# Newton steps and scaled x of a norm in PSUM, norms interleaved with the products that remain, and copies moved between engines, in a two-layer hybrid diffusion backbone

## Chip, cores and metric

One NeuronCore of one Trainium2 chip. The metric is the device time of one execution in microseconds, the median of several runs. Most executions of one kernel agree within 0.3%.

## What is computed

Two layers run over 512 latent tokens and 256 context tokens of width 1024, in fp32:

```python
for l in range(2):
    sh1, sc1, g1, sh2, sc2, g2 = modulation(c, ada_w[l], ada_b[l], 6)   # silu(c) @ ada_w + ada_b
    # the context has its own six from c_ctx; in the last layer only the first two
    hx = modulate(x, norm1_g[l], sh1, sc1)        # rms_norm(x, g) * (1 + scale) + shift
    hc = modulate(xc, norm1_g[l], csh1, csc1)
    ux, uc = hx @ w_in[l], hc @ w_in[l]           # keys, values, queries, pool input, gates
    # mixers: multi-scale pooling, 2-D neighbourhood attention, windowed attention with sinks,
    # latent attention; latent queries read latent and context keys, context reads context only
    mixed = sum(sigmoid(gate_i) * (y_i @ w_branch[i])) @ w_out
    x = x + g1 * mixed
    x = x + g2 * ((silu(h @ w1) * (h @ w3)) @ w2)    # h = modulate(x, norm2_g, sh2, sc2)
    # the context stream gets the same two updates, except in the last layer
return rms_norm(x, final_norm_g)
```

## The kernel before

Activations lie transposed: eight tiles of 128 channels by 768 tokens, 512 latent ones (piece `PL`) and 256 context ones (piece `PC`). Each fp32 operand is split in a high part and the rest, and a product is three matmuls (`mm3`, L149 to L151): high x high, rest x high, high x rest. A weight slab is loaded by SyncE's queue into `wraw` (three buffers), converted by ScalarE to the high part (L143) and subtracted by GpSimd to the rest (L157; the tiles `gatelo`, `wolo`, `w1lo` and so on; four buffers each).

The order of TensorE's work is made by a `Stream` of jobs. A job is a generator that emits some matmuls and then yields the microseconds that they should take; when a job starts, the weights of the next one are loaded. `st.defer(us, fn, key)` has `fn` emitted once the jobs have passed that much product time, `st.need(key)` emits it at once. Attention is emitted between pieces of jobs (`st.drive`). The framework then lays out each engine's queue ahead of the run: earlier emitted instructions come first when their inputs should be ready. SyncE's queue keeps the emitted order.

The parts that the change touches:

- **adaLN work.** `ada_run(n)` takes n steps of the generator that computes the modulation vectors. After the first four groups, a group is eight loads of a 128x512 weight block (`adaraw`) with one or two VectorE products each into PSUM (`adaacc`, tag `sc`; L397, L399), and a transpose and a reduction for each accumulator (L406, L407). Nine `adaraw` blocks have room, and up to eight are loaded ahead. `cur["side"]` is the number of steps for each four k tiles of a product, from the second job of the fourth gate on 1.2, in the FFN 0.75. Layer 0's second norm needs groups up to the sixth.
- **Norm.** `Norm.squares` adds up squares as x is updated (L468, L469). `stats` sums over channels on TensorE (`ps_ssq`, L476), computes the reciprocal root by three Newton rounds on columns (`newton`, L442 to L448, VectorE) and writes a diagonal `dg` (L480). `apply` spreads it by a matmul (`ps_rstd`, L487), then per k scales x on VectorE (`nh`, L514), adds the shift on ScalarE (L517, L521) and writes the two halves `hh` and `hl` (L519 by GpSimd or VectorE, L522 by VectorE).
- **PSUM.** Eight banks: tag `mm` three, `sc` two, `tr` two, `pv` one. `ps_ssq` and `ps_rstd` take `tr`; so do output products of the second piece.
- **Projections.** `project_jobs` has eight output tiles m. For the output projection (b = 16) and the last part of w2 (b = 40), tiles 4 to 7 do the first piece only, and four `tail` jobs then do the rest. `stats(first)` follows the first tail, `apply(first)` the second. The pieces are `PL`, `PC` in layer 0 and two halves of 256 tokens in layer 1.
- **First FFN job.** `first_ffn_job` does hidden tile 0 for the first piece, then the other piece's norm, then that piece.
- **Entry of layer 1.** `mix` emits the pool products, and after them the context norm's `apply` and the token-major products (`tm`).
- **Mixers.** `split_k` puts each key half into both partition halves (L956, L957); the pool branch sums windows (L741, L743); `na_bias` adds a mask to a bias block in three instructions per head (L1010).

## Time and profile before

| | us |
|---|---|
| Median of 3 runs | 2248.66 (2248.55 to 2250.43) |
| The profiled execution, among them | 2250.43 |
| Its span | 2248.6 |

| Engine | busy us | share of the span |
|---|---|---|
| TensorE, matmuls | 2153.3 | 96% |
| VectorE | 1298.7 | 58% |
| ScalarE | 878.3 | 39% |
| GpSimd | 723.7 | 32% |

The granted TensorE clock was 0.985 of full speed over the span. In the rows, PE is TensorE, PEld its weight loads, DVE VectorE, ACT ScalarE, POOL GpSimd, SPq the load queue of SyncE. Times in a row of instructions are from the span's start; L is a line of the kernel.

### The profile page before, as it was taken

To read this page: it belongs to the slowest core of one execution; us is meant where nothing else is said; L and a number is where in the kernel's file an instruction comes from. 1 tells how busy PE (TensorE), PEld (TensorE's weight loads), DVE (VectorE), ACT (ScalarE), POOL (GpSimd) and SP (SyncE) were. 2 spreads that over 40 slices of the span, in tenths; PEclk is the share of its full clock that TensorE was granted. 3 is DMA by queue.
4 is the path that set the end of the run, shared out by engine and by line. 5 is a ranking of instruction groups with operands and counts; after the bars stand their busy time and mean duration, and the time that the engine had idled before them with its cause. 6 is when DMAs were issued, how large, how long until landed. Compare 5 with 4: busy or idle time off the path is not lost.

```text
span 2248.6 us, 32590 instructions
## 1 busy us (share of the span) xinstructions
PE 2153.3 (96%) x11792; PEld 1840.8 (82%) x11792; DVE 1298.7 (58%) x2935; ACT 878.3 (39%) x1973; POOL 723.7 (32%) x591
## 2 busy tenths in 40 slices
PE   6999999999999899999999998998999988999998
PEld 2878888888888788888888877877887787888886
DVE  6774667767789877644412266667777444212225
ACT  4354555544432422122122334555655334323233
POOL 1322222222222323333333323323233353444443
PEclk9999999999999899999999999999999999999999
DMA  7422111112454334445422223322222232333332
GB/s 240 111 60 57 43 50 43 45 45 64 125 166 147 109 124 140 141 133 154 126 69 60 89 83 103 87 57 59 59 66 69 82 115 64 98 95 96 99 100 89
DMA packets 317333, 211.59 MB, mean 94 GB/s; under 512 B 17370, under 2 KB 284916, under 8 KB 317172
## 3 DMA queue, kind: packets, MB, share of 16 engines
q1 hardware_dynamic: 308756, 201.65, 31.1%
q10 hardware_dynamic: 8416, 7.87, 1.0%
q8 instruction: 93, 1.52, 0.3%
q14 instruction: 68, 0.56, 0.1%
HBM read 202.90 MB, written 6.55 MB: 93 GB/s over the span
## 4 chain that ended last, share of the span: by engine, by line
PE 77%; DVE 12%; DMA 3%; ACT 2%; issue 2%; POOL 1%; SPq 0%; ACTq 0%; POOLq 0%; DVEq 0%
PE ps_w L150 13%; PE ps_w L149 13%; PE ps_w L151 13%; PE ps_gate L149 5%; PE ps_gate L151 5%; PE ps_gate L150 5%; PE pv L869 3%; PE tr L855 2%; DMA gater<-in_w_in_dram 1%; DVE adaacc L399 1%; PE ps_y L149 1%; PE ps_y L150 1%; PE ps_y L151 1%; PE ps_wo L151 1%; PE ps_wo L150 1%
## 5 line engine op out<-in xcount | busy, mean ns | idle before, releaser
L157 POOL TENSOR_TENSOR gatelo<-gater,gatehi 128x512 fp32r<-128x512 f32 x128 | 172.5, 1351 | 461.0 <-ACT gatehi L143 439.4
L149 PE MATMUL ps_gate<-hh,gatehi 128*128 128x512 f32 (+1 forms) x768 | 278.9, 363 | 1.4 <-ACT gt L808 1.4
L151 PE MATMUL ps_gate<-hh,gatelo 128*128 128x512 f32 (+1 forms) x768 | 274.3, 357 | 0.8 <-POOL gatelo L157 0.6
L150 PE MATMUL ps_gate<-hl,gatehi 128*128 128x512 f32 (+1 forms) x768 | 274.0, 357 | 0.0
L399 DVE SCALAR_TENSOR_TENSOR adaacc<-adaraw,cs,adaacc 128x512 f32<-128x512 f32 x224 | 160.5, 749 | 77.3 <-DMA adaraw<-in_ada_w_dram 76.2
L149 PE MATMUL ps_w<-hh,w1hi 128*128 128x512 f32 (+1 forms) x504 | 179.4, 356 | 0.0
L149 PE MATMUL ps_w<-hh,w3hi 128*128 128x512 f32 (+1 forms) x504 | 178.7, 355 | 0.0
L150 PE MATMUL ps_w<-hl,w1hi 128*128 128x512 f32 (+1 forms) x504 | 178.5, 354 | 0.0
L150 PE MATMUL ps_w<-hl,w3hi 128*128 128x512 f32 (+1 forms) x504 | 178.5, 354 | 0.0
L151 PE MATMUL ps_w<-hh,w1lo 128*128 128x512 f32 (+1 forms) x504 | 178.3, 354 | 0.0
L151 PE MATMUL ps_w<-hh,w3lo 128*128 128x512 f32 (+1 forms) x504 | 178.3, 354 | 0.0
L157 POOL TENSOR_TENSOR w3lo<-w3r,w3hi 128x512 fp32r<-128x512 f32 x84 | 110.6, 1322 | 191.1 <-ACT w3hi L143 189.3
L157 POOL TENSOR_TENSOR w1lo<-w1r,w1hi 128x512 fp32r<-128x512 f32 x84 | 108.6, 1294 | 190.2 <-ACT w1hi L143 187.6
L149 PE MATMUL ps_w<-gh,w2hi 128*128 128x512 f32 (+1 forms) x472 | 165.6, 351 | 0.0
L151 PE MATMUL ps_w<-gh,w2lo 128*128 128x512 f32 (+1 forms) x472 | 165.3, 350 | 0.0
L150 PE MATMUL ps_w<-gl,w2hi 128*128 128x512 f32 (+1 forms) x472 | 165.2, 350 | 0.0
L151 PEld LDWEIGHTS ps_gate<-hh,gatelo 128*128 128x128 f32 x768 | 145.5, 189 | 21.6 <-POOL gatelo L157 1.6
L149 PEld LDWEIGHTS ps_gate<-hh,gatehi 128*128 128x128 f32 x768 | 145.7, 190 | 19.7 <-ACT gt L808 2.3
L150 PEld LDWEIGHTS ps_gate<-hl,gatehi 128*128 128x128 f32 x768 | 146.0, 190 | 16.9
L157 POOL TENSOR_TENSOR w2lo<-w2r,w2hi 128x512 fp32r<-128x512 f32 (+1 forms) x80 | 97.5, 1224 | 157.1 <-ACT w2hi L143 155.7
L1497 DVE SCALAR_TENSOR_TENSOR ft<-ft,ps_w 128x512 f32<-128x512 f32 (+1 forms) x67 | 39.4, 589 | 145.5 <-ACT ft L1496 145.4
L143 ACT ACTIVATE gatehi<-gater 128x512 fp32r<-128x512 f32 x128 | 80.4, 630 | 96.9 <-DMA gater<-in_w_in_dram 33.6
(420 smaller groups left out, 5615.3 us busy)
## 6 DMA issues: line engine op xcount, KB each, us to landing
adaraw<-in_ada_w_dram SPq DMA_DIRECT2D x160, 256.0 KB
gater<-in_w_in_dram SPq DMA_DIRECT2D x128, 256.0 KB
w1r<-in_ffn_w_dram SPq DMA_DIRECT2D x84, 256.0 KB
w3r<-in_ffn_w_dram SPq DMA_DIRECT2D x84, 256.0 KB
w2r<-in_ffn_w_dram SPq DMA_DIRECT2D x56, 256.0 KB
ada<-in_ada_w_dram SPq DMA_DIRECT2D x32, 256.0 KB
wbr<-in_w_branch_dram SPq DMA_DIRECT2D x64, 128.0 KB
wor<-in_w_out_dram SPq DMA_DIRECT2D x32, 256.0 KB
```

What stands on the lines that cost most here:

```text
L143: nc.scalar.activation(out=o, in_=i, func=AF.Copy, scale=scale)
L149: nc.tensor.matmul(ps, ah, bh, start=start, stop=False)
L150: nc.tensor.matmul(ps, ah, bl, start=False, stop=False)
L151: return nc.tensor.matmul(ps, al, bh, start=False, stop=stop).ins
L157: cur["lo"].tensor_tensor(out=lo, in0=raw, in1=hi.bitcast(F32), op=ALU.subtract)
L399: nc.vector.scalar_tensor_tensor(out=acc[j], in0=raw, scalar=c, in1=acc[j], op0=ALU.mult, op1=ALU.add)
L855: nc.tensor.transpose(tr[:, 128 * j:128 * j + 128], ps[qi][0][:, c0:c0 + 128], ident)
L869: nc.tensor.matmul(acc[:, 128 * q0:128 * (q0 + nq)], v[rows], t[rows, c:c + 128 * nq], start=(i == 0), stop=(i == nmm - 1))
L1497: nc.vector.scalar_tensor_tensor(out=t, in0=t, scalar=1.0, in1=p1, op0=ALU.add, op1=ALU.mult)
```

## The change

The Newton steps keep `y` and the shifted integer in the columns behind the sums, in the same PSUM bank. The scaled x of `apply` goes to PSUM (tag `sc`, two banks) and every k takes the two-instruction form. `stats` and `apply` of the first piece are deferred by 2.0 and 5.5 us from the end of the last tile's first piece. The first FFN job becomes six: hidden tile 0 and hidden tile 1 for the first piece, tile 1 and then tile 0 for the second. The context norm at the entry to layer 1 is deferred by 2.0 us into the pool products. adaLN steps run at 1.4 in place of 1.2 and stop at six groups until hidden tile 1 is done for the first piece. Squares are deferred by 1.5 us. One key copy and the pool branch's copy go from VectorE to ScalarE, the bias additions from VectorE to GpSimd, and two of four heads' bias blocks are loaded and added 24 us later.

```diff
@@ -179,7 +179,7 @@
     st = Stream()
-    cur = {"ada": None, "side": 0.0, "credit": 0.0, "groups": 0, "after": None, "lo": nc.gpsimd, "wants": (1.3, 2.0, 1.3, 1.4)}
+    cur = {"ada": None, "cap": 6, "side": 0.0, "credit": 0.0, "groups": 0, "after": None, "lo": nc.gpsimd, "wants": (1.3, 2.0, 1.3, 1.4)}
@@ -194,7 +194,8 @@
                     cur["credit"] -= 1
-                    ada_run(1)
+                    if cur["groups"] + (cur["ada"] is not None) < cur["cap"]:
+                        ada_run(1)
                 yield min(n, step) * 3 * (s1 - s0) / 2400
@@ -435,13 +436,16 @@
-    def newton(src, n, mean):
+    def newton(src, n, mean, room=None):
         v, y, t = (cp.tile([128, 8], F32, tag=f"nw{c}", name=f"nw{c}", bufs=2)[:, :n] for c in "vyt")
+        g = t
+        if room is not None:
+            y, g = room[:, 0:n], room[:, n:2 * n]
         V = nc.vector
         V.tensor_scalar(out=v, in0=src, scalar1=mean, scalar2=EPS, op0=ALU.mult, op1=ALU.add)
-        V.tensor_scalar(out=t.bitcast(I32), in0=v.bitcast(I32), scalar1=1, scalar2=None, op0=ALU.logical_shift_right)
-        V.tensor_scalar(out=y.bitcast(I32), in0=t.bitcast(I32), scalar1=-1, scalar2=0x5F3759DF, op0=ALU.mult, op1=ALU.add)
+        V.tensor_scalar(out=g.bitcast(I32), in0=v.bitcast(I32), scalar1=1, scalar2=None, op0=ALU.logical_shift_right)
+        V.tensor_scalar(out=y.bitcast(I32), in0=g.bitcast(I32), scalar1=-1, scalar2=0x5F3759DF, op0=ALU.mult, op1=ALU.add)
         for _ in range(3):
@@ -471,10 +475,10 @@
         nt = n // 128
-        ps = psum("tr", "ps_ssq", 2 * nt)
+        ps = psum("tr", "ps_ssq", 6 * nt)
         for t in range(nt):
             nc.tensor.matmul(ps[:, 2 * t:2 * t + 2], acc[:, 128 * t:128 * t + 128], ones[:, 0:2], start=True, stop=True)
-        r = newton(ps, 2 * nt, mean)
+        r = newton(ps[:, 0:2 * nt], 2 * nt, mean, ps[:, 2 * nt:6 * nt])
         dg = tmp([128, n], F32, "dg")
@@ -510,16 +514,11 @@
                 sh, sc = (mods[self.l][:, b + k, cond:cond + 1] for b in self.b)
-                t = tmp([128, n], F32, "nh")
+                t = psum("sc", "nh", n)
                 nc.vector.scalar_tensor_tensor(out=t, in0=cur["x"][k][:, s0:s1], scalar=sc, in1=rstd, op0=ALU.mult, op1=ALU.mult)
                 hh, hl = (t_[:, s0:s1] for t_ in cur["h"][k])
-                if k % 2:
-                    nc.scalar.activation(out=t, in_=t, func=AF.Identity, bias=sh)
-                    act_copy(hh, t)
-                    (nc.gpsimd if k == 1 else nc.vector).tensor_tensor(out=hl, in0=t, in1=hh.bitcast(F32), op=ALU.subtract)
-                else:
-                    nc.scalar.activation(out=hh, in_=t, func=AF.Identity, bias=sh)
-                    nc.vector.scalar_tensor_tensor(out=hl, in0=t, scalar=sh, in1=hh.bitcast(F32), op0=ALU.add, op1=ALU.subtract)
+                nc.scalar.activation(out=hh, in_=t, func=AF.Identity, bias=sh)
+                nc.vector.scalar_tensor_tensor(out=hl, in0=t, scalar=sh, in1=hh.bitcast(F32), op0=ALU.add, op1=ALU.subtract)
@@ -740,7 +739,7 @@
                     if j >= both:
-                        nc.vector.tensor_copy(dst[0:64, 8:n + 8], prev[0:64, 8:n + 8])
+                        act_copy(dst[0:64, 8:n + 8], prev[0:64, 8:n + 8])
                     prev = dst
@@ -953,7 +952,7 @@
                 sub_hi(dst[1], src, dst[0])
-                nc.vector.tensor_copy(kd[e][o, s0:s1], kd[e][r, s0:s1].bitcast(F32))
+                act_copy(kd[e][o, s0:s1], kd[e][r, s0:s1].bitcast(F32))
                 nc.vector.tensor_copy(kl[e][o, s0:s1], kl[e][r, s0:s1].bitcast(F32))
@@ -1007,7 +1006,7 @@
                 for v, (j0, nj) in enumerate(((8, 24), (0, 32), (0, 24))):
-                    nc.vector.tensor_tensor(out=bt[:, v, :nj, :], in0=raw[:, :, j0:j0 + nj].rearrange("p r j -> p j r"),
+                    nc.gpsimd.tensor_tensor(out=bt[:, v, :nj, :], in0=raw[:, :, j0:j0 + nj].rearrange("p r j -> p j r"),
                                             in1=nam[:, v, :nj, :], op=ALU.add)
@@ -1327,8 +1326,9 @@
                 norm.stats(PC)
+                st.defer(2.0, lambda: norm.apply(PC), "norm")
                 st.until(jobs[0], False)
-                norm.apply(PC)
+                st.need("norm")
                 tm = tm_jobs()
@@ -1337,7 +1337,7 @@
             v0, v1 = v
-            bias += [na_bias(2 + e, nam) for e in range(2)]
+            st.defer(24.0, lambda: bias.extend(na_bias(2 + e, nam) for e in range(2)), "bias")
             y_na = [pair("y", TQ, "yn") for _ in range(2)]
@@ -1349,6 +1349,7 @@
             st.until(g)
+            st.need("bias")
             _, qs0 = swa_q_job(0, tab)
@@ -1416,7 +1417,7 @@
             if m == 1 and not last:
-                cur["side"] = 1.2
+                cur["side"] = 1.4
             if m:
@@ -1454,7 +1455,7 @@
                         nm[0] = new_norm()
-                    nm[0].squares(m, p)
+                    st.defer(1.5, lambda: nm[0].squares(m, p), p)
@@ -1466,18 +1467,29 @@
                     kept[m] = w_
+                if not last and b == 16 and m == KD - 1:
+                    ada_until(6)
+                    cur["side"] = 0.0
+                elif new_norm and b == 40 and m == 0:
+                    ada_run(1000)
+                    cur["side"] = 0.0
                 yield from go(m, w_, (first,) if late else (first, *rest))
+                if late and m == KD - 1:
+                    st.defer(2.0, stats)
+                    st.defer(5.5, apply, "norm")
+            def stats():
+                st.need(first)
+                nm[0].stats(first)
+            def apply():
+                cur["h"] = new_h()
+                nm[0].apply(first)
...
                 yield from go(m, kept[m], rest)
-                if m == 4:
-                    nm[0].stats(first)
-                elif m == 5:
-                    cur["h"] = new_h()
-                    if not last and b == 16:
-                        ada_until(6)
-                        cur["side"] = 0.0
-                    nm[0].apply(first)
+                if m == KD - 1:
+                    st.need("norm")
@@ -1499,21 +1511,49 @@
-        def first_ffn_job(g):
-            def run(w):
+        def first_ffn_jobs(g):
+            held = {}
+            def first(w):
+                held[0] = w
                 g.append(pair("q", TQ, "g"))
-                for i, p in enumerate(split):
-                    ps = [psum("mm", "ps_w13", p[1] - p[0]) for _ in range(2)]
-                    if i == 0:
-                        nm2[0].stats(split[1])
-                    yield from together(ps, w, p)
-                    if i == 0:
-                        nm2[0].apply(split[1])
-                    swiglu(g[0], *ps, p)
-                cur["side"] = 0.0 if last else 0.75
-                cur["after"] = cur["last"]
-            return st.add(run, lambda: [slab(a[n][l], 0, "w13", keep="y") for n in ("ffn_w1", "ffn_w3")])
+                ps = [psum("mm", "ps_w13", split[0][1] - split[0][0]) for _ in range(2)]
+                st.defer(1.0, stats, "stats")
+                yield from together(ps, w, split[0])
+                st.need("stats")
+                nm2[0].apply(split[1])
+                swiglu(g[0], *ps, split[0])
+            def stats():
+                st.need(split[1])
+                nm2[0].stats(split[1])
+            def one(i, q, w=None):
+                if w:
+                    held[1 + i] = w
+                if i == 0 and q == 0:
+                    g.append(pair("q", TQ, "g"))
+                held["ps", i] = psum("mm", "ps_w13", split[q][1] - split[q][0])
+                yield from mm_piece(held["ps", i], held[1 + i], cur["h"], split[q])
+                if i:
+                    swiglu(g[1], held["ps", 0], held["ps", 1], split[q])
+                    if q == 0:
+                        cur["side"], cur["cap"] = 0.0 if last else 0.75, 99
+                        cur["after"] = cur["last"]
+            def second(_):
+                ps = [psum("mm", "ps_w13", split[1][1] - split[1][0]) for _ in range(2)]
+                yield from together(ps, held[0], split[1])
+                swiglu(g[0], *ps, split[1])
+            st.add(first, lambda: [slab(a[n][l], 0, "w13", keep="y") for n in ("ffn_w1", "ffn_w3")])
+            for i, n in enumerate(("ffn_w1", "ffn_w3")):
+                st.add(lambda w, i=i: one(i, 0, w), lambda n=n: slab(a[n][l], 128, "w13"))
+            for i in range(2):
+                st.add(lambda _, i=i: one(i, 1))
+            st.add(second)
@@ -1633,8 +1673,8 @@
                 if hc0 + j == 0:
-                    first_ffn_job(g)
-                else:
+                    first_ffn_jobs(g)
+                elif hc0 + j > 1:
                     ffn_jobs(128 * (hc0 + j), g, j)
@@ -1648,8 +1688,6 @@
         norm = nm[0]
-        ada_run(1000)
-        cur["side"] = 0.0
         xst = dp.tile([KD, 128, NX], F32, name="xst")
```

## Rows read from the trace of the kernel before

**Rows 1.** Stretches: from:to, length, busy us (count) of each engine, granted clock, DMA.
```profile
core 0: us, PE busy (x) PEld busy (x) DVE busy (x) ACT busy (x) POOL busy (x), PEclk, DMA share, GB/s
742.00:790.00 48.00, 38.61 (x213) 33.48 (x213) 43.53 (x95) 20.96 (x40) 12.77 (x10) 0.86 0.33 96
1318.00:1367.00 49.00, 44.53 (x231) 37.90 (x230) 41.33 (x98) 24.35 (x48) 17.54 (x14) 0.97 0.21 55
1845.00:1890.00 45.00, 36.40 (x239) 33.22 (x238) 27.50 (x74) 18.90 (x43) 13.29 (x11) 0.89 0.17 47
651.00:663.00 12.00, 11.34 (x66) 9.91 (x66) 12.00 (x20) 4.32 (x10) 5.05 (x5) 1.00 0.67 198
```
**Rows 2.** TensorE's waits, whole span: line <- releaser: us in total, times, longest.
```profile
PE ps_rstd L487 <- DVE dg L480: 12.9, 7, 4.5
```
**Rows 3.** The same, 742 to 790 us.
```profile
PE ps_rstd L487 <- DVE dg L480: 4.5, 1, 4.5
...
PE ps_ssq L476 <- DVE acc L469: 1.4, 2, 0.7
PE ps_wo L149 <- DVE x L1453: 0.9, 1, 0.9
```
**Rows 4.** The same, 1845 to 1890 us.
```profile
PE ps_rstd L487 <- DVE dg L480: 5.1, 2, 3.0
PE ps_w L150 <- POOL hl L519: 1.3, 2, 1.0
```
**Rows 5.** The same, 1318 to 1367 us.
```profile
PE ps_tm L149 <- DVE pwr L712: 2.0, 1, 2.0
PE ps_rstd L487 <- DVE dg L480: 1.5, 1, 1.5
```
**Rows 6.** VectorE in order of time, layer 0's second norm: start, us, instruction.
```profile
747.96 0.15 DVE L442 TENSOR_SCALAR nwv<-ps_ssq 128x8 f32<-128x8 f32 x1
...
749.09 0.75 DVE L399 SCALAR_TENSOR_TENSOR adaacc<-adaraw,cs,adaacc 128x512 f32<-128x512 f32 x1
...
754.15 1.69 DVE L480 TENSOR_SCALAR dg<-ident,nwy 128x128 f32<-128x128 f32 x3
```
**Rows 7.** VectorE and GpSimd in order of time, layer 1's second norm.
```profile
1852.11 1.28 POOL L157 TENSOR_TENSOR w13lo<-w13r,w13hi 128x512 fp32r<-128x512 f32 x1 [0.99 <-ACT w13hi L143]
1852.17 1.24 DVE L447 TENSOR_TENSOR nwt<-nwt,nwy 128x4 f32<-128x4 f32 x1
...
1869.95 0.16 DVE L442 TENSOR_SCALAR nwv<-ps_ssq 128x4 f32<-128x4 f32 x1 [0.70 <-PE ps_ssq L476]
...
1872.33 0.48 DVE L480 TENSOR_SCALAR dg<-ident,nwy 128x128 f32<-128x128 f32 x2
1874.13 0.48 DVE L514 SCALAR_TENSOR_TENSOR nh<-x,mod,ps_rstd 128x256 f32<-128x256 f32 x1 [1.32 <-PE ps_rstd L487]
```
**Rows 8.** By tile nh and hl, 755 to 775 and 1872 to 1882: ns min/median/max.
```profile
L514 DVE SCALAR_TENSOR_TENSOR nh<-x,mod,ps_rstd x8: 734/743/748, 759.3 to 768.8; 128x512 f32<-128x512 f32 x8
L521 ACT ACTIVATE hh<-nh,mod x4: 710/716/727, 760.1 to 768.3; 128x512 fp32r<-128x512 f32 x4
L522 DVE SCALAR_TENSOR_TENSOR hl<-nh,mod,hh x4: 741/752/1120, 761.3 to 769.5; 128x512 fp32r<-128x512 f32 x4
...
L522 DVE SCALAR_TENSOR_TENSOR hl<-nh,mod,hh x4: 477/479/480, 1875.3 to 1879.2; 128x256 fp32r<-128x256 f32 x4
```
**Rows 9.** SyncE's load queue in order of time, output projection of layer 0.
```profile
715.52 10.14 SPq L372 DMA_DIRECT2D adaraw<-in_ada_w_dram  x3
725.75 0.94 SPq L163 DMA_DIRECT2D wor<-in_w_out_dram  x2
```
**Rows 10.** TensorE in order of time, seventh output tile (m = 6) of layer 0.
```profile
731.37 0.39 PE L149 MATMUL ps_wo<-mhh,wohi 128*128 128x512 f32 x1
731.60 0.39 PE L150 MATMUL ps_wo<-mhl,wohi 128*128 128x512 f32 x1
```
**Rows 11.** By tile bias (whole span) and hl (1872 to 1882 us): ns min/median/max.
```profile
L1010 DVE TENSOR_TENSOR bias<-braw,nam x24: 470/512/1483, 95.6 to 1409.9; 128x192 f32<-128x192 f32 x16, 128x256 f32<-128x256 f32 x8
...
L519 POOL TENSOR_TENSOR hl<-nh,hh x1: 828/828/828, 1876.3 to 1876.3; 128x256 fp32r<-128x256 f32 x1
```

## The prediction

> **What bounds the kernel now.** I read the stretch view first, then TensorE's waits, then the instructions in order of time inside three stretches. Between norms TensorE hardly pauses, so other engines' work counts only where TensorE ends up waiting. Around layer 0's second norm (742 to 790 us) TensorE is busy 38.6 of 48 us, 9.4 idle, and its mean granted clock is 0.86, which is at most 0.14 x 48 = 6.7 us of full-rate time. Around layer 1's second norm (1845 to 1890) it is idle 8.6 us at 0.89, another 5.0 at most. At the entry to layer 1 (1318 to 1367) it is idle 4.5 at 0.97, another 1.5 [rows 1]. [...] The total of the waits says what is late: TensorE waits 12.9 us in seven places for the diagonal `dg`, the end of the Newton chain [rows 2]; 4.5 of it in layer 0's second norm [rows 3], 5.1 in layer 1's [rows 4], 1.5 at the entry [rows 5].
>
> Why `dg` is late differs. In layer 0 the Newton steps, begun at 747.96, take turns on VectorE with adaLN products of 0.75 us until 754.15, and the `dg` writes then last 1.69 for three of them [rows 6]. In layer 1 there are no adaLN products, but a step on four columns lasts 1.24 us while a GpSimd split of 1.28 us runs; undisturbed, twelve steps go from 1869.95 to 1872.33, 2.4 us [rows 7].
>
> **Part by part.** *Newton in PSUM.* `y` and the shifted integer move to the bank of the sums, so no step has two SBUF tensors. If the long steps come from two engines wanting SBUF together, the 1.24 us step falls back to the 0.2 of the quiet chain; three such steps in a chain are 3 us, all of layer 1's first `dg` wait (3.0 [rows 4]). `dg` itself stays SBUF to SBUF and can still be caught. No row has a small step that writes PSUM. The nearest are the adaLN products, which read and write PSUM in 0.75 us [rows 6], against 0.743 and 0.752 for SBUF results of the same size [rows 8]. I take 0; the bounds are 0.1 us saved or lost per step (half of a quiet step), 1.2 per chain. [...]
>
> *Bank of the sums.* It is now held until `dg` is read, not until the first step: some 3 us of one of two `tr` banks. In layer 0 the third tail product then has to wait for the addition behind the second; before pays such a wait once, 0.9 [rows 3].
>
> *Scaled x in PSUM, one form for all k.* Per piece and k there remain one scaling, one ScalarE pass, one difference. Four ScalarE passes and one GpSimd difference per application go, one VectorE difference comes. VectorE then needs 8 x (0.743 + 0.752) = 12.0 us for 512 columns and, with as much for a scaling as for a difference, 8 x 0.96 = 7.7 for 256 [rows 8]. What goes is the blocking by GpSimd (a difference of 0.75 took up to 1.12). Two banks suffice while ScalarE's 0.716 and two handovers fit beside one scaling and one difference (1.5 us).
>
> *adaLN rate 1.4, cap 6.* The six groups that the norm needs are due after 61 steps: 1.4 x 44 credit points is 61.6, so the last comes at the end of the fourth output product instead of during the eighth, and nothing of group 7 starts before the second hidden tile. So the adaLN products leave the Newton chain, and its 6.2 us (747.96 to 754.15) become 2.4. Price: 0.8 step more per gate job, two products of 0.75 each, 1.2 us, on a VectorE that is already full (12.00 of 12.00 us in one gate job [rows 1]). It would fall some 5 us behind by the fourth output product. Queued behind it are SP's loads: three adaLN loads hold SP 10.14 us until slots are free, and the weights behind them are issued at 725.75 [rows 9] for products that start at 731.37 [rows 10]; transfer, conversion and split have 5.6 us there, and need some 4.5. I take 2 us lost; bounds 0 and 8 (weights late at two products).
>
> *Stats and application deferred, FFN products interleaved.* `stats` stays behind the first tail product; `rstd` moves from behind the second to the middle of the third, a half product of 12 matmuls of 0.12 (half of 0.23 at 512 columns [rows 10]), 1.4 us of cover. The other piece's norm gets two products of the next hidden tile as cover, 48 matmuls: 11 us in layer 0, 5.8 in layer 1, on top of the first tile's own 11 or 5.8. The number of matmuls is unchanged. That norm's chain: addition, square, accumulation and sums 2.5 (four instructions of about 0.48 and handovers), Newton to first scaling 1869.95 to 1874.13, 4.2 [rows 7], application 7.7, SwiGLU between 1.5: about 16. Layer 0 covers 22, so nothing stays. Layer 1 covers 11.6 and wants the last k 2.5 later, 14: 2 late, up to 4 if VectorE must finish the first half before.
>
> *Entry of layer 1.* The context norm is applied 2 us into the pool products, ahead of the pool chain on VectorE rather than mixed with it; the `tm` products' 2.0 us wait [rows 5] is for a place in that queue.
>
> *Mixers.* The key copy goes from VectorE to ScalarE. The bias additions (24, median 0.512) go to GpSimd, at about 0.83 by its own 256-column difference [rows 11], some 2.3 us per head in front of weight splits; two of four heads move 24 us later. Bounds: 8 us gained (the mixers' waits for keys and pool products) to 5 lost (a split late by 2.3 at two heads); I take 3 gained. The pool copies on ScalarE and the deferred squares are hidden by the products that run; without that cover each is 0.4 to 0.7 us.
>
> **Sum.** Layer 0's second norm: of 16.1 us (9.4 + 6.7) there stay 0.7 for the sums [rows 3], 0.9 for the bank, 1.1 for the first `hl` and a quarter of the clock's loss, 1.7: 4.4. 11.7 go, less 2 for the adaLN rate: 9.7. Layer 1's: of 13.6 there stay 1.5 at the first half, 3 at the second, 1.7 of clock; 7.4 go. Entry: of 6.0 the 2.0 of `tm` and 2 of the rest go, 4. Mixers 3. Together 24 us. The profiled execution took 2250.43, its span 2248.6 and 1.8 around it, and is 1.8 above the median of 2248.66. 2250.4 - 24 = 2226.4; against the median 2224.7. I say 2226.
>
> **Rivals.** *Half comes* (2235 to 2244, at 2240): VectorE stays the late engine. Its long instructions are as many as before, so the wait for `dg` turns into one for `hl`; output weights come 6 us later than I take in layer 0, by the SP queue; layer 1's halves stay 4 late; the entry's pool chain is late instead: 24 - 6 - 4 - 4 = 10. For it: VectorE full in the gate job [rows 1]. Against: 3 us of contended steps and 4 of shared turns have nothing to do with its length [rows 6, 7].
>
> *Nothing measurable* (near 2249): the norms go as meant, but GpSimd's bias work and the held `tr` bank give it back in the attention stages: 24 additions at 0.83 are 20 us of GpSimd, of which TensorE would have to see nearly all. Against: weights are split a product ahead, and GpSimd is busy a third of the span.
>
> *Slower* (near 2255): two PSUM banks for the scaled x, where seven SBUF tiles stood. If VectorE's order is scaling k, then its difference, one k costs 0.743 + 0.716 + 0.752 and two handovers, 2.4 us, not 1.5. TensorE eats a k of two 512-column products in six matmuls, 1.4 us, so both 512 applications add 8; at 256 columns a k costs 1.75, and layer 1's two halves add some 7 each: 30 in all, 24 - 30, 6 slower. It decides as soon as ScalarE's answer, with weight conversions in its queue, takes longer than one scaling and one difference. Against: with two banks one scaling can always stand ahead.
>
> **How the numbers follow.** Forecast 0.55 (2212 to 2235), half 0.24, nothing 0.08, slower 0.13. The low end, 2208, has the 8 of the mixers, no lost weight and the clock's 3.4 back too (24 + 5 + 2 + 3.4 = 34, and most of what is left at layer 1); the high end, 2248, takes in the first rival and the edge of the second, so that the slower case and little below the low end stay out. About 0.2% (4.5 us) is what a measurement of this kernel can tell from no change; faster by more is 0.55 + 0.24 = 0.79, within 0.08, slower 0.13.
>
> **What would show it.** Right: TensorE's waits for `dg` total below 6 us; no adaLN product stands between Newton steps of layer 0's second norm and no step lasts over 0.3; scaling and difference alternate with no idle VectorE; no gap before hidden tile 1's second piece in layer 0; mean clock of the three stretches above 0.95. Wrong: TensorE waits for `wohi`, `wolo` or a `wor` load between 700 and 745, or for `gatelo` behind a bias addition; VectorE idle for `hh` inside an application; over 4 us of waits for `hl` at tile 1's second piece in layer 1.

## The result, and the profile after

| | us |
|---|---|
| Kernel before, median of 4 runs | 2248.61 (2244.63 to 2250.43) |
| Changed kernel, median of 4 runs | 2219.71 (2218.82 to 2223.32) |
| Ratio | 0.9868, 95% interval 0.9857 to 0.9880 |
| Profiled execution of the changed kernel, its span | 2220.52, 2218.7 |

The change is worth 28.9 us; 24 were forecast (2226, range 2208 to 2248). The total is near, but it came from other places than the sum had it, so that the nearness is in part luck. The start of one and the same product in both traces (us) gives the gain stage by stage:

| Product | before | after | gained in the stage | forecast |
|---|---|---|---|---|
| layer 0, first output product | 686.5 | 678.8 | 7.7 | mixers, both layers: 3 |
| layer 0, w1 of hidden tile 3 | 823.4 | 812.9 | 2.8 | 9.7 |
| layer 1, last token-major quarter (ps_tm) | 1367.7 | 1353.6 | 3.5 | entry: 4 |
| layer 1, first output product | 1807.9 | 1786.9 | 6.9 | (mixers) |
| layer 1, w1 of hidden tile 2 | 1895.5 | 1865.2 | 9.3 | 7.4 |

A stage's gain is known to some 2 us: five kernels of this document that have the same code up to the first output product of layer 0 begin it between 678.5 and 680.3 in their traces.

Stretches of the changed kernel that answer to [rows 1], with the first mixers of layer 0 ahead (from:to, length, busy us and count of TensorE, its weight loads, VectorE, ScalarE, GpSimd, then the granted clock):

```profile
100.00:140.00 40.00, 34.12 (x193) 29.56 (x192) 32.94 (x78) 24.33 (x56) 14.68 (x13) 0.96 0.24 59
734.00:780.00 46.00, 43.49 (x247) 38.05 (x246) 35.28 (x82) 17.78 (x34) 10.60 (x8) 0.96 0.15 44
780.00:810.00 30.00, 24.04 (x145) 21.80 (x144) 28.71 (x51) 5.82 (x12) 7.87 (x6) 0.89 0.66 201
1306.00:1354.00 48.00, 44.76 (x249) 39.50 (x247) 39.54 (x99) 22.41 (x42) 14.37 (x12) 1.00 0.22 57
1825.00:1862.00 37.00, 35.63 (x286) 34.66 (x285) 27.98 (x80) 17.98 (x39) 14.65 (x12) 1.00 0.25 72
```

In layer 0's norm (734 to 780) TensorE idles 2.5 us where it idled 9.4, and in layer 1's 1.4 where it idled 8.6. But the stretch just behind, 780 to 810, has 6 us of idle time at a clock of 0.89; in the kernel before TensorE was busy without a break from 790 to 820, at 1.00. TensorE's waits over the whole span name it:

```profile
PE ps_w L149 <- DVE ft L1509: 6.0, 1, 6.0
...
PE ps_wo L149 <- DVE dg L484: 3.1, 2, 2.4
...
PE ps_rstd L491 <- DVE dg L484: 2.5, 4, 1.0
```

The 12.9 us for `dg` of [rows 2] are 5.6 now, 3.1 of them under another name: an output product waits for the bank that `dg` is read from. The new entry is the 6.0 us for `ft`, the SwiGLU's tile (ScalarE writes a tanh to it, VectorE multiplies it with the two products). The mean granted clock was 0.985 of 2248.6 us before and 0.992 of 2218.7 after, in the profiled executions; that is 33.7 and 17.7 us of full-rate time lost, 16 apart. Over all executions whose clock is on record the mean is 0.987 (34 of the kernel before) and 0.991 (four of the changed one), 28.7 and 20.5 us. So 8 to 16 of the 30 us are clock that came back; that it came back behind the waits that went or grew short is argued from where those stretches lie.

### The profile page after: what moved, and what is told of

Its sections match the earlier page's. It is cut to its first block, busy times and chain, and to the rows that moved or that the text cites. A ratio compares the mean times of both kernels' runs of the same rounds, so it can differ in the third digit from the quotient of the medians.

```text
span 2218.7 us, 32705 instructions
## 1 busy us (share of the span) xinstructions
PE 2138.8 (96%) x11840; PEld 1835.8 (83%) x11840; DVE 1270.4 (57%) x2890; ACT 883.5 (40%) x1981; POOL 732.7 (33%) x609
## 3 DMA queue, kind: packets, MB, share of 16 engines
q8 instruction: 93, 1.52, 0.3%
## 4 chain that ended last, share of the span: by engine, by line
PE 80%; DVE 9%; DMA 3%; ACT 3%; issue 2%; POOL 1%; ACTq 0%; SPq 0%; DVEq 0%; POOLq 0%
PE ps_w L149 13%; PE ps_w L150 13%; PE ps_w L151 13%; PE ps_gate L149 6%; PE ps_gate L150 6%; PE ps_gate L151 6%; PE pv L868 3%; PE tr L854 2%; PE ps_y L149 1%; PE ps_y L150 1%; PE ps_y L151 1%; PE ps_wo L151 1%; DMA gater<-in_w_in_dram 1%; PE ps_wo L149 1%; PE ps_wo L150 1%
## 5 line engine op out<-in xcount | busy, mean ns | idle before, releaser
L149 PE MATMUL ps_w<-hh,w1hi 128*128 128x512 f32 (+1 forms) x480 | 171.6, 358 | 6.0 <-DVE ft L1509 6.0
L150 PE MATMUL ps_w<-hl,w1hi 128*128 128x512 f32 (+1 forms) x480 | 170.7, 356 | 0.0
L151 PE MATMUL ps_w<-hh,w1lo 128*128 128x512 f32 (+1 forms) x480 | 170.5, 355 | 0.0
L149 PE MATMUL ps_w<-hh,w3hi 128*128 128x512 f32 (+1 forms) x480 | 170.3, 355 | 0.0
L150 PE MATMUL ps_w<-hl,w3hi 128*128 128x512 f32 (+1 forms) x480 | 170.0, 354 | 0.0
L151 PE MATMUL ps_w<-hh,w3lo 128*128 128x512 f32 (+1 forms) x480 | 169.8, 354 | 0.0
L157 POOL TENSOR_TENSOR w1lo<-w1r,w1hi 128x512 fp32r<-128x512 f32 x80 | 103.8, 1299 | 196.2 <-ACT w1hi L143 194.2
L157 POOL TENSOR_TENSOR w3lo<-w3r,w3hi 128x512 fp32r<-128x512 f32 x80 | 105.1, 1321 | 187.8 <-ACT w3hi L143 186.7
```

The lines of the kernel that those rows point to most:

```text
L149: nc.tensor.matmul(ps, ah, bh, start=start, stop=False)
L150: nc.tensor.matmul(ps, ah, bl, start=False, stop=False)
L151: return nc.tensor.matmul(ps, al, bh, start=False, stop=stop).ins
L157: cur["lo"].tensor_tensor(out=lo, in0=raw, in1=hi.bitcast(F32), op=ALU.subtract)
```

## Experiments

Every ratio is to the kernel before, run beside it on the same chip; 0.001 is 2.2 us.

### The SwiGLU behind the adaLN products

```diff
                 if i:
                     swiglu(g[1], held["ps", 0], held["ps", 1], split[q])
-                    if q == 0:
-                        cur["side"], cur["cap"] = 0.0 if last else 0.75, 99
-                        cur["after"] = cur["last"]
...
                 swiglu(g[0], *ps, split[1])
+                cur["side"], cur["cap"] = 0.0 if last else 0.75, 99
+                cur["after"] = cur["last"]
```

> The changed kernel, but adaLN work starts again only after hidden tile 0's second piece, not after tile 1's first piece. In the changed kernel's trace TensorE waits 6.0 us at 794 us for the SwiGLU of that piece, whose VectorE instruction stands from 788.2 (ScalarE's tanh) to 799.6 behind a row of adaLN products, and the half-rate stretch 797 to 804 follows. Theory (credit): two products walked k tile by k tile earn one credit each 24 matmuls of 0.12 us eight times instead of twice, 16 x 0.75 = 12 steps of two products of 0.75 us, 18 us of VectorE in 5.8 us of TensorE; without them the wait goes (6.0) and 3.4 of clock: about 2210 to 2212, no wait for ft above 1 us between 770 and 820. Rival (VectorE is full anyhow): the adaLN work that is owed only moves later, the wait appears in the next hidden tile or at the end of layer 0: 2217 to 2221.

Measured: 2212.16, ratio 0.9832 (0.9818 to 0.9845), 7.5 us less than the changed kernel. The wait for `ft` is gone, and nothing takes its place from 770 to 1300 us, up to the end of layer 0; the theory holds. What stood in the way, in order of time on ScalarE (first line) and VectorE of the changed kernel:

```profile
788.17 0.39 ACT L1508 ACTIVATE ft<-ps_w 128x256 f32<-128x256 f32 x1 [4.10 <-PE ps_w L151]
```
```profile
784.49 5.35 DVE L400 SCALAR_TENSOR_TENSOR adaacc<-adaraw,cs,adaacc 128x512 f32<-128x512 f32 x8
789.76 1.30 DVE L407 STREAM_TRANSPOSE adat<-adaacc 128x512 f32<-128x512 f32 x2
790.99 1.23 DVE L408 TENSOR_REDUCE adapart<-adat 128x16 f32<-128x512 f32 x2
792.14 1.39 DVE L398 TENSOR_SCALAR adaacc<-adaraw,cs 128x512 f32<-128x512 f32 x2
...
796.35 3.38 DVE L400 SCALAR_TENSOR_TENSOR adaacc<-adaraw,cs,adaacc 128x512 f32<-128x512 f32 x5
799.64 0.41 DVE L1509 SCALAR_TENSOR_TENSOR ft<-ft,ps_w 128x256 f32<-128x256 f32 x1
```

The tanh begins at 788.2; VectorE's next instruction on `ft` starts at 799.6, since VectorE has adaLN work without a break from 784.5 on. `together` walks two products side by side, k tile by k tile, and the credit (`cur["side"]`), meant for four k tiles, is paid for each.

### Newton steps in SBUF

```diff
-        ps = psum("tr", "ps_ssq", 6 * nt)
+        ps = psum("tr", "ps_ssq", 2 * nt)
...
-        r = newton(ps[:, 0:2 * nt], 2 * nt, mean, ps[:, 2 * nt:6 * nt])
+        r = newton(ps, 2 * nt, mean)
```

> The changed kernel with the Newton steps back in SBUF, all else as it is. Theory (contention): a step with two SBUF tensors is held up by GpSimd's SBUF work, as the 1.24 us step beside a 1.28 us split in the kernel before; single steps of 0.9 to 1.3 us come back, two or three in a chain that meets a split, and the norms' dg comes 2 to 3 us later where nothing covers it: 2222 to 2228. Rival (order, not memory): the steps were slow because adaLN products and copies stood between them, and these are gone; no step above 0.3 us, 2218 to 2221.

Measured: 2222.46, ratio 0.9880 (0.9865 to 0.9895): 2.7 us more, at the low edge of the theory's range, and the intervals overlap a little, so the time alone does not settle it. The lengths of the steps decide between theory and rival. VectorE and GpSimd in layer 1's second norm, Newton in SBUF:

```profile
1831.08 1.17 DVE L448 TENSOR_SCALAR nwy<-nwt 128x4 int32<-128x4 int32 x1
...
1833.27 1.25 DVE L452 SCALAR_TENSOR_TENSOR nwy<-nwt,nwy 128x4 f32<-128x4 f32 x1
1834.55 0.16 DVE L450 SCALAR_TENSOR_TENSOR nwt<-nwy,nwv 128x4 f32<-128x4 f32 x1
1834.75 1.19 DVE L451 TENSOR_TENSOR nwt<-nwt,nwy 128x4 f32<-128x4 f32 x1
...
1836.17 0.48 DVE L484 TENSOR_SCALAR dg<-ident,nwy 128x128 f32<-128x128 f32 x2
```
```profile
1830.92 1.30 POOL L157 TENSOR_TENSOR w13lo<-w13r,w13hi 128x512 fp32r<-128x512 f32 x1 [0.15 <-ACT w13hi L143]
1833.21 2.72 POOL L157 TENSOR_TENSOR w13lo<-w13r,w13hi 128x512 fp32r<-128x512 f32 x2 [0.99 <-ACT w13hi L143]
```

Each long step stands beside one GpSimd split, three splits and three steps. The same norm in the changed kernel, with a split of 1.30 us at 1829.95:

```profile
1830.30 0.16 DVE L450 SCALAR_TENSOR_TENSOR nwt<-ps_ssq,nwv 128x4 f32<-128x4 f32 x1
1830.50 0.16 DVE L451 TENSOR_TENSOR nwt<-nwt,ps_ssq 128x4 f32<-128x4 f32 x1
...
1832.07 1.52 DVE L484 TENSOR_SCALAR dg<-ident,ps_ssq 128x128 f32<-128x128 f32 x2
```
```profile
1829.95 1.30 POOL L157 TENSOR_TENSOR w13lo<-w13r,w13hi 128x512 fp32r<-128x512 f32 x1 [0.15 <-ACT w13hi L143]
```

No step is longer than 0.17, and the chain is 2.4 us instead of 5.5. But `dg`, still SBUF to SBUF, meets the next split: 1.52 for two writes, and 2.74 for four in layer 0. From the first step to the last `dg`, PSUM saves 2.1 us in layer 1 and 1.1 in layer 0. That is near the 2.7 us but does not explain them: between the starts of the products in the table above the two kernels take as long, 134.0 and 134.1 us in layer 0's norm and 78.0 and 78.3 in layer 1's. What grew most is TensorE's wait for `dg` at the entry to layer 1 (1290 to 1362 us), 0.8 in the changed kernel and with Newton in SBUF

```profile
PE ps_rstd L491 <- DVE dg L484: 3.6, 2, 3.4
```

Where the 2.7 us arise the traces do not settle.

### The scaled x in SBUF, and the order of the SwiGLU

The first kernel puts `apply` back to SBUF tiles and its two forms (the lines that the change removes there); the second is the first with one more edit:

```diff
-                t = psum("sc", "nh", n)
+                t = tmp([128, n], F32, "nh")
```
```diff
                 st.need("stats")
-                nm2[0].apply(split[1])
                 swiglu(g[0], *ps, split[0])
+                nm2[0].apply(split[1])
```

> The changed kernel with the scaled x of a norm in SBUF again and two forms for odd and even k, as before. Recorded theory: the eight scalings and differences of an application are as long in either place (0.743 and 0.752 at 512 columns, 0.48 at 256), and what returns is the blocking by GpSimd (a difference of 0.75 took up to 1.12, in the kernel before one took 1.76) and one GpSimd difference per application of 0.83 to 1.74 us: 1 to 4 us over all norms, 2221 to 2224, with hl or nh instructions above 1.1 us and a wait of TensorE for hl on GpSimd. Rival (the banks serialise): two PSUM banks hold the scalings back behind ScalarE, so that seven SBUF tiles are the better place: 2214 to 2219.

> The changed kernel with the scaled x in SBUF and two forms (2233 alone, 13 us above the changed kernel), and hidden tile 0's SwiGLU of the first piece written ahead of the second piece's application, not behind it. In the trace with SBUF alone ScalarE stands idle for 6.1 us in front of the application's first shift at 1855.9, with the tanh of a finished product behind it in its queue, and TensorE waits 6.0 us for that product's bank; in layer 0 twice 2 us. Theory (order): in PSUM the two banks made the application look slow to the layout of the queues, which let the SwiGLU go first, and that, not the place of x, is most of the 13 us: 2219 to 2225, no wait for ft in layer 1, and that of 3.8 in layer 0 halved. Rival (place): SBUF itself costs it, by GpSimd's difference and blocked instructions: 2229 to 2234.

Measured: 2233.17 (0.9924, 0.9911 to 0.9938) for SBUF alone, 13.5 us above the changed kernel and far above both expectations; 2227.52 (0.9904, 0.9887 to 0.9920) with the SwiGLU ahead, between theory and rival, with intervals that overlap a little. By the starts of the products in the table above, SBUF alone loses 2.5 us in layer 0's second norm and 10.8 in layer 1's. ScalarE in layer 1's second norm, SBUF alone, and TensorE's wait there:

```profile
1855.91 0.51 ACT L525 ACTIVATE hh<-nh,mod 128x256 fp32r<-128x256 f32 x1 [6.14 <-DVE nh L518]
...
1860.20 0.64 ACT L1513 ACTIVATE ft<-ps_w 128x256 f32<-128x256 f32 x2
```
```profile
PE ps_w L149 <- DVE ft L1514: 6.0, 1, 6.0
```

and ScalarE in the changed kernel:

```profile
1846.33 0.39 ACT L1508 ACTIVATE ft<-ps_w 128x256 f32<-128x256 f32 x1 [2.11 <-PE ps_w L151]
...
1850.27 0.83 ACT L520 ACTIVATE hh<-nh,mod 128x256 fp32r<-128x256 f32 x2
```

In ScalarE's queue with seven SBUF tiles nearly the whole application stands ahead of the tanh, and ScalarE waits 6.1 us for the norm while a finished product holds its bank. With two PSUM banks the tanh goes first. That the layout chooses so by the number of buffers, and not by the longer two-form application, is not shown. Writing the SwiGLU first takes the 6.0 us wait away (none for `ft` in layer 1) and 5.6 of the 13.5 us; layer 0's waits for `ft`, expected to halve from 3.8, are 4.2. Of the rest, layer 1's norm has 4.8 us by the start of its tile 2: waits for `hl` of 2.4 us, 1.2 of them on GpSimd's difference, where the changed kernel has 0.4, and 0.7 for the sums. Some 3 us stay unplaced, and no run separates the place of x from its two forms. The instructions themselves are as long as in the kernel before [rows 8], and none is blocked any more (tile `nh`, changed kernel: ns least/median/most):

```profile
L518 DVE SCALAR_TENSOR_TENSOR nh<-x,mod,ps_rstd x48: 473/483/756, 749.5 to 1856.5; 128x256 f32<-128x256 f32 x32, 128x512 f32<-128x512 f32 x16
...
L521 DVE SCALAR_TENSOR_TENSOR hl<-nh,mod,hh x48: 469/478/753, 751.3 to 1858.5; 128x256 fp32r<-128x256 f32 x32, 128x512 fp32r<-128x512 f32 x16
```

### The mixers' edits

Alone on the kernel before (bias additions on GpSimd and half of them later, key and pool copies on ScalarE), and undone by halves on the changed kernel:

```diff
-                act_copy(kd[e][o, s0:s1], kd[e][r, s0:s1].bitcast(F32))
+                nc.vector.tensor_copy(kd[e][o, s0:s1], kd[e][r, s0:s1].bitcast(F32))
```
```diff
-                    nc.gpsimd.tensor_tensor(out=bt[:, v, :nj, :], ...
+                    nc.vector.tensor_tensor(out=bt[:, v, :nj, :], ...
```

> The kernel before with the mixers' edits alone: bias additions on GpSimd, two heads' bias 24 us later, key copy and pool copy on ScalarE. The recorded sum gives the mixers 3 us: about 2246, within 2244 to 2249. The changed kernel's trace, set against that of before, shows some 6 us gained up to the gates of layer 0 and some 9 to 10 between the context norm and the latent attention of layer 1. If the edits named here make that (theory: VectorE is relieved where keys and pool products wait for it), 2233 to 2238. If it is the Newton steps in PSUM that made it (the mixers' own norms wait for dg), 2243 to 2247, and the waits for k, 1.5 and 1.0 us, are gone all the same.

> The changed kernel with the key copy and the pool copy back on VectorE. Theory A (the bias additions made most of the mixers' 11 us): 2219 to 2222. Theory B (the copies did): the waits of TensorE for k (1.5 and 1.0 at the first head of layer 1, 1.0 in layer 0 in the kernel before) are back, with 1.7 us of clock for each half-rate stretch behind them, 2224 to 2228.

> The changed kernel with the 24 bias additions back on VectorE and all four heads' bias loaded at once. The mixers' edits alone were worth 11 us (0.995 of the time before). Theory A (the additions: they stand on VectorE among the pool sums and in front of keys and queries, 24 x 0.512 = 12.3 us of it, a good half of that in the two first heads of a layer): 4 to 8 us come back, 2224 to 2228. Theory B (the copies: the waits of TensorE for k, 1.5 + 1.0 + 1.0, and the clock behind them made the gain): 2219 to 2222 here.

Measured: the edits alone 2239.52 (0.9950, 0.9938 to 0.9963), 10.6 us gained and a little short of the expected 12 or more; copies undone 2226.06 (0.9898, 0.9884 to 0.9911), 6.3 us lost; bias undone 2220.42 (0.9875, 0.9862 to 0.9889), nothing that can be told from zero. So the copies carry most of it; the key copy and the pool copy were not tried one by one. With both undone the first output product of layer 0 starts at 684.2, 5.4 us behind the changed kernel's 678.8, and the profiled spans are 5.6 apart: by these traces the loss arises in layer 0's mixers. The 40 us from 100 in layer 0, in the order before, edits alone, copies undone:

```profile
100.00:140.00 40.00, 32.16 (x163) 27.09 (x163) 35.31 (x90) 18.12 (x42) 11.94 (x8) 0.87 0.24 60
```
```profile
100.00:140.00 40.00, 34.27 (x195) 29.79 (x195) 33.23 (x77) 23.20 (x52) 14.98 (x13) 0.91 0.23 59
```
```profile
100.00:140.00 40.00, 32.90 (x157) 27.88 (x156) 31.84 (x77) 15.83 (x38) 14.49 (x13) 0.83 0.23 59
```

TensorE's busy time differs little, but the count of its instructions and the clock do: 0.83 with the copies on VectorE, 0.96 in the changed kernel, 5.2 us of full-rate time (3.2 against the 0.91 of the edits alone). TensorE's waits there, copies undone:

```profile
PE ps_pw L149 <- DVE ypl L766: 3.7, 1, 3.7
PE ps_nak L149 <- ACT pb L143: 2.4, 1, 2.4
PE sc L917 <- ACT k L143: 1.0, 1, 1.0
```

In the kernel before the three read 3.9, 2.2 and 1.0, in the changed one 4.6, 1.2 and nothing, with the edits alone 4.6, 1.1 and nothing. The pool branch's `pb` comes sooner, and the wait for a key, which follows right behind the longest one, is gone. The waits alone are 1.3 us (7.1 against 5.8); the clock is the larger part. In layer 1 the expected waits for keys, 1.5 and 1.0, did not come back (0.4 in one place).

### adaLN rate and due time

```diff
-                cur["side"] = 1.4
+                cur["side"] = 1.2
...
-                if not last and b == 16 and m == KD - 1:
-                    ada_until(6)
-                    cur["side"] = 0.0
-                elif new_norm and b == 40 and m == 0:
+                if new_norm and b == 40 and m == 0:
...
             def apply():
                 cur["h"] = new_h()
+                if not last and b == 16:
+                    ada_until(6)
+                    cur["side"] = 0.0
```

> The changed kernel with adaLN work at 1.2 steps instead of 1.4 and the six groups demanded where the norm is applied, not ahead of the last output product; nothing of a seventh group starts before hidden tile 1 is through, as in the changed kernel. Recorded theory: the last groups' products then stand among the Newton steps of layer 0's second norm and in front of its application, 3.8 us of chain and 1.7 to 3.4 of clock, less up to 2 that the higher rate costs in the gate products: 2221 to 2227, with a wait of TensorE for dg or for hh between 740 and 760. Rival (covered): the deferred norm has the tail products as cover, and the products end in time: 2217 to 2221.

Measured: 2220.82 (0.9872, 0.9856 to 0.9887): no difference. The rival holds, and TensorE's waits say why: 1.8 us for output weights (593 to 745) that the changed kernel has and this one has not,

```profile
PE ps_wo L149 <- ACT wohi L143: 1.0, 1, 1.0
PE ps_wo L151 <- POOL wolo L157: 0.8, 2, 0.5
```

are made up by a new wait of 1.0 for the first `hh` (between 740 and 760) and 0.8 more for `ft`. The run keeps the cap of six groups, and in its trace too no adaLN product stands among the Newton steps (740.55 to 742.97). In the kernel before the products among them belong to a seventh group, begun behind the last transposition of the sixth (740.24):

```profile
740.87 0.71 DVE L397 TENSOR_SCALAR adaacc<-adaraw,cs 128x512 f32<-128x512 f32 x1
```

So it should be the cap that clears the chain; no run here takes the cap away.

### One job for the first hidden tile

`first_ffn_job` of the kernel before in place of the six jobs, so that adaLN work also starts after it:

```diff
-                    first_ffn_jobs(g)
-                elif hc0 + j > 1:
+                    first_ffn_job(g)
+                else:
```

> The changed kernel with the first hidden tile as one job again (tile 0 first piece, then second piece), so hidden tile 1 no longer stands in front of the second piece; adaLN work starts after it, as in the kernel before. Theory (cover): the second piece's norm shows again, dg and the first hh and hl, 3 to 4 us and 1.7 of clock in layer 0, 4 to 5 us and up to 5 of clock in layer 1; the 6.0 us wait for the SwiGLU and its 3.4 of clock go: between 2219 and 2226, taken at 2222, with waits of TensorE for dg or hh at both second pieces. Rival (no cover needed): with short Newton chains and an unblocked application the second piece is in time without it, and what is left is the gain of the SwiGLU wait: 2209 to 2213.

Measured: 2214.99 (0.9843, 0.9830 to 0.9857), between theory and rival and 4.7 us less than the changed kernel, which has the adaLN work too early. Against the kernel with that mended (2212.16) the interleaving is worth 2.8 us, and the intervals overlap. The waits at the second pieces without it, layer 0 and then layer 1:

```profile
PE ps_w L149 <- ACT hh L520: 1.3, 1, 1.3
```
```profile
PE ps_w L149 <- ACT hh L520: 1.1, 1, 1.1
PE ps_rstd L491 <- DVE dg L484: 1.0, 1, 1.0
```

3.4 us were left for it to cover, not the 14 to 16 of the whole chain.

### The places of the sums and applications

Sums behind the first tail product, application behind the second, squares at once, and the context norm at the entry to layer 1 behind the pool products, all as before:

```diff
-                st.defer(2.0, lambda: norm.apply(PC), "norm")
...
-                st.need("norm")
+                norm.apply(PC)
...
-                    st.defer(1.5, lambda: nm[0].squares(m, p), p)
+                    nm[0].squares(m, p)
...
-                if m == KD - 1:
-                    st.need("norm")
+                if m == 4:
+                    stats()
+                elif m == 5:
+                    apply()
```

> The changed kernel with the sums and the application of the first piece behind the first and second tail product as before, the squares at once, and the context norm at the entry to layer 1 behind the pool products as before. Recorded theory: the entry's context norm alone is 4 us, by the wait for a place in VectorE's queue at the token-major products, and rstd in front of a whole product instead of in the middle of one 1.4 us of cover in each norm: 2222 to 2227, with the entry's waits (1318 to 1367 of the kernel before: 4.5 us idle) mostly back. Rival (the short Newton chains leave nothing to cover): 2218 to 2221, no wait at the entry above 1 us.

Measured: 2218.84 (0.9870, 0.9852 to 0.9888): no difference. At the entry TensorE waits 4.4 us (2.5 of them for `ps_rstd`, 1.5 for the evacuation of a `q`), in the changed kernel 3.2 (1.7 for `ps_rstd`, 1.2 for `hl`), but that does not reach the end. The rival's time holds, though not its waits, which were to stay below 1 us. Where the norms are written makes no gain that can be measured.

### The held bank, and who writes `dg`

```diff
-        ps = psum("tr", "ps_ssq", 6 * nt)
+        ps = psum(tag, "ps_ssq", 6 * nt)
...
-            self.dg[piece] = rstd_diag(self.acc[:, s0:s1], s1 - s0, 1.0 / D)
+            self.dg[piece] = rstd_diag(self.acc[:, s0:s1], s1 - s0, 1.0 / D, "pv" if self.b[0] else "tr")
```

> The changed kernel with adaLN work starting after tile 0's second piece (2212 alone) and the sums and Newton columns of the second norms in the bank that attention uses for its products with v, not in one of the two transposition banks. In the changed kernel the third tail product waits 2.4 us in layer 0 and 0.8 in layer 1 until dg is read and the bank is free, and a half-rate stretch of 3.4 us follows the first. Theory (held bank): 2.4 + 0.8 + 1.7 of clock go: 2206 to 2209. Rival (dg itself is late, the rows of rstd come next and need it): the wait moves from the tail product to rstd, 2210 to 2213.

Measured: 2211.02 (0.9831, 0.9816 to 0.9846), the same as without it. The wait for the bank went and the wait for `dg` came, in layer 0 and layer 1:

```profile
PE ps_rstd L491 <- DVE dg L484: 2.0, 1, 2.0
```
```profile
PE ps_rstd L491 <- DVE dg L484: 0.9, 1, 0.9
```

So the bank was not the cause, `dg` was: here too its four writes last 2.98 us from 743.54. The last kernel lets the last Newton step write an SBUF tile, from which ScalarE takes its scale, and ScalarE write `dg`:

```diff
+            if act:
+                i = nc.scalar.activation(out=o, in_=ident, func=AF.Copy, scale=s)
+            else:
                 i = nc.vector.tensor_scalar(out=o, in0=ident, scalar1=s, scalar2=None, op0=ALU.mult)
```

> The changed kernel with adaLN work starting after tile 0's second piece (2212 alone), and in the second norms the last Newton step written to SBUF and the diagonal dg written by ScalarE instead of VectorE; the sums stay in a transposition bank, which is free again before dg is written. With the sums in another bank alone (2211) the wait of the third tail product, 2.4 and 0.8, only turned into waits of 2.0 and 0.9 for dg itself: four writes of 0.28 last 2.98 us in layer 0 while GpSimd splits a weight. Theory (VectorE held by GpSimd's SBUF work): ScalarE writes four in about 1.2 us (0.30 for a 128x128 conversion), so 2 of the 2.4 us, most of 0.8 and the half-rate stretch of 3.4 us (1.7) go: 2206 to 2209. Rival (dg is late whoever writes it, since conversions stand in ScalarE's queue, or the next wait is for the first hh): 2210 to 2214.

Measured: 2207.68, ratio 0.9812 (0.9793 to 0.9832): as the theory had it, 4.5 us below the kernel with the late adaLN work alone (the intervals overlap a little) and the fastest here, 40.7 us below the kernel before. TensorE waits for nothing between 735 and 830 (in layer 1 a wait of 1.0 for the first `hh` of the second piece is left), and the four writes are

```profile
742.75 1.28 ACT L487 ACTIVATE dg<-ident,nwv 128x128 f32<-128x128 f32 x4 [0.31 <-DVE nwv L453]
```

## Why the prediction was right, step by step

**What bounds it** held: the waits for `dg`, slow Newton steps, a mean clock below one in the norms' stretches. The sum's terms for clock suppose that a pause that goes takes lost clock along; no run shows how much of it goes with a pause. What the traces show is the means: 0.86 and 0.89 before [rows 1], 0.96 and 1.00 after, which is 1.8 us (0.04 x 46) and nothing left, where 1.7 and 1.7 were taken to stay; 3.3 more (0.11 x 30) are lost in the stretch behind the first, 780 to 810. In the kernel with the mended adaLN work layer 0's norm gains 11.1 us by the same two products as in the table above (first output product 6.2, tile 3's w1 17.3), and 11.7 were forecast for it ahead of the adaLN price. The signs named for "right" came: waits for `dg` of 5.6, no adaLN product among the Newton steps, no step over 0.3, no gap ahead of the second piece in layer 0, clocks of 0.96, 1.00 and 1.00. Of the signs for "wrong" there is little: waits of 0.3 us for `wolo` between 700 and 745 and of 0.9 for `gatelo` in two places (0.6 in one before), and VectorE idle for `hh` 2.0 us in six places.

**Newton in PSUM.** Contention was the right reason [rows 7]: put back, steps of 0.97 to 1.28 us return. Zero for a PSUM step was the right choice: least, median and most over 39 steps of 4 and 8 columns are 144, 157 and 164 ns for the product, which reads `y` in PSUM, and 152, 167 and 171 for the step that writes it there, where quiet steps in SBUF take 0.16. The size was off: 2.7 us in all, which the traces do not place, not 3 in layer 1's norm alone. There `dg` is caught in the steps' stead, as feared in half a sentence and not priced.

**The bank.** 0.9 was forecast for layer 0, measured 2.4, and 0.8 in layer 1. The term was taken from a wait for another cause [rows 3]; its size was that of `dg`'s blocked writes.

**Scaled x.** The slower rival (two banks serialise, 30 us) was wrong in sign. Its condition, that ScalarE answers later than one scaling and one difference, did not come about (VectorE idles 2.0 us for `hh` in all, 0.7 at most); the chain's instructions are 0.48 and 0.75 as forecast. What the sum had not at all is that such a change also alters the order in which the queues are laid out: the old application in SBUF costs 13.5 us, 5.6 of them by that order.

**adaLN.** The price of the higher rate, 2 us by late output weights, came: waits for them total 1.8 from 593 to 745, 1.5 of it at the first output product, where the kernel before and the one at the old rate have none. The slack behind it was read too large: from the load's issue at 725.75 to the end of its first split at 731.63 the kernel before took 5.9 us, not some 4.5, which was an estimate. What the rate was to buy, a Newton chain without adaLN products, is there with the old rate too, under the cap, and the total is the same. What the clear chain is worth, taken for 3.8 us, no run measures. The step that failed is a missing one: the prediction followed the cap up to its lifting and did not count what the lifted rate pays inside `together`. That is the 6.9 us by which layer 0's norm fell short (9.7 forecast, 2.8 measured); with the lifting put later, 7.5 us come back.

**Cover.** Right in direction, too large: the second piece's chain of 14 to 16 us was to be hidden, but with the adaLN products and long steps gone only 3.4 us of it showed.

**Entry.** 3.5 measured, 4 forecast, but not for the reason given: the place of the context norm moves nothing that can be measured. The Newton steps are the likelier reason, by the 3.6 and 0.8 us of waits for `dg` above.

**Mixers.** Forecast 3, measured 10.6 for their edits alone. It lies outside the bounds (8 gained, 5 lost): the 8 were the mixers' waits alone, without the clock (0.87 in the 40 us from 100 before, 0.91 with the edits alone), and the 5 a late split behind the bias additions. The additions are worth nothing measurable, and the copies, of which the text gave the key copy no price and called the pool copies hidden, 6.3. The term that failed is this one: the copies stand in front of two products beside the longest wait of the stretch, and the clock is lower as well (0.83 with them on VectorE, 0.96 in the changed kernel). These 7 us more than forecast stand against the 6.9 less of layer 0's norm, which helped the total to come out near.

The parts undone one at a time do not add up to 28.9 us: 13.5, 6.3, 2.7, 1.1 and 0.7 lost, and 4.7 (one job, with the adaLN work mended) and 0.9 (the places) gained. About 10 us belong to no single part. That where one cover is gone another still works is a guess; pairs were not tried.

## What to carry to other kernels

Before a rate or a cap is lifted, count what it pays in every loop that hands out work in another step, and look at what then stands in the queue ahead of the next bank's reader. If an engine's queue is laid out by estimates, a change of an application's buffers or form can also be a change of order: compare the queues, not only the prices of the instructions. Beside a GpSimd split small VectorE steps here took 0.16 to 0.17 us with `y` in PSUM, and with it in SBUF 1.17 to 1.25: on a critical chain it pays to place them where a split does not lengthen them, and the last of them, here the diagonal, as much as the first (four writes took 2.74 us on VectorE, 1.28 on ScalarE).

## What the runs showed of the hardware

A VectorE instruction with a single SBUF input was long beside GpSimd's work as well: an integer step took 1.17 us for 0.17, a `dg` write 1.32 for 0.28, each beside a split of 1.3, and each ended within 0.1 us of the split's end; with operand and result in PSUM the integer step stayed at 0.17 beside such a split. The `dg` writes on ScalarE took 0.70 for two and 1.28 for four, though GpSimd split a weight from 742.51 to 743.81 beside the four. By what path GpSimd holds VectorE no run shows.

Waits and clock in the 40 us from 100, run by run: with waits of 2.4, 3.7 and 1.0 us the mean was 0.83 (copies undone), with 2.2, 0.7, 3.9 and 1.0 it was 0.87 (before), with 0.7, 0.5 and 4.1 and with 1.1 and 4.6 it was 0.91 (bias undone, the edits alone), and with 1.2 and 4.6 it was 0.96 (changed). More waits went with a lower mean, but nearly the same waits gave 0.91 and 0.96, so the waits are not all that decides.
